# Attention scores of a two-layer mixer: products on two row tiles of 64 partitions instead of full-height products of 96

## The chip, the cores and the metric

The kernel runs on one core of a Trainium2 chip. The metric is device time of one execution in microseconds (us), the median of several executions. A core has five engines with an instruction stream each: TensorE (PE in the profile; PEld is its weight load, which is a row of its own), VectorE (DVE), ScalarE (ACT), GpSimd (POOL) and SyncE (SP), which here issues the DMAs. Engines wait for one another by semaphores.

## The reference, cut to what matters

Two layers work on 2048 latent and 256 context tokens of width 1024. The first is a convolution with a state-space scan. The second is multi-head attention with 16 heads: a head's query and key have 64 channels without position (`nope`) and 32 rotary channels (`rope`), and the rotary channels of the key are shared by all heads. The 2048 latent queries attend to all 2304 keys, 18 blocks of 128.

```python
q = jnp.concatenate([q_nope, q_rope], axis=-1)            # 64 + 32 channels
k = jnp.concatenate([k_nope, k_rope_of_all_heads], axis=-1)
...
s = jnp.einsum('bqhd,bkhd->bhqk', qblk, k, preferred_element_type=F32) * scale
p = jax.nn.softmax(s, axis=-1)
return jnp.einsum('bhqk,bkhv->bqhv', p.astype(v.dtype), v)
...
out_l = (att_l.reshape(b_, n, MLA_MIX) * jax.nn.silu(g_l)) @ w_out
```

## The kernel before

The change touches the attention of the second layer. Single precision is had from split operands: a number is a rounded high part and a low part, and `mm3` makes a product from three matmuls, high by high, high by low and low by high. Queries, keys and values, already split, lie in DRAM (`qd`, `qrd`, `kd`, `krd`, `vd`) before the attention starts.

The work runs over 64 pairs of a head and a block of 512 queries. For each pair, `NP` = 9 steps run over two key blocks of 128 each, so there are 64 x 9 = 576 steps. The loop at the end of the kernel writes each engine's instructions in that order by hand (a manual schedule); a step holds work of several lags:

- `scores`: for each of the two key blocks one `mm3` into its bank of the PSUM tile `s` (lines 119 to 121). The weights are a key block [96, 128], the moving operand is the query block [96, 512]. These are six matmuls of 96 rows and 512 columns.
- `evac_s` (ACT copies `s` to `S`, L1929), `run_max` (DVE, L1941), then 12 to 16 steps later `sub` (DVE, L1970), `exp_` (ACT, L1975), `p_hi` (ACT or POOL, L1985, L1983), `p_lo` (POOL, L1991).
- `pv`: 18 short half-precision matmuls of the probabilities by the values into `O` (L2011).
- in step 1 of a pair `max_a`, four transposes (L1951), in step 3 `max_b`, four more (L1965). `finish` divides by the row sum (DVE, L2018 to L2025; POOL, L2027).
- `side()`: at the three `side_step` calls of a step it yields one `mm3` of 512 columns into `fps`: gates and output projections. A job is 8, 4 or 2 such products with one `at` tile, which is fetched from DRAM one job ahead.

`load_k` brings a head's keys in three tiles `K` of six blocks, in steps 1, 4 and 7 of the pair before the head changes; there are four buffers. `load_qt` brings a query block one pair ahead. Each of the two issues two DMAs, one for the 64 nope rows and one for the 32 rope rows, with high and low parts side by side in a tile. All these DMAs stand in the one queue of SP, in order.

Of the kernel before, what the change touches and what calls it, by code (L numbers as in the profile page):

```python
# [10 lines left out]
F32 = mybir.dt.float32  # L11
F32R = mybir.dt.float32r
# [3 lines left out]
ALU = mybir.AluOpType  # L16
# [4 lines left out]
P = 128  # L21
# [12 lines left out]
NOPE = 64  # L34
ROPE = 32
QD = 96
VH = 64
QL = 384
# [19 lines left out]
def hybrid_conv_s5_mla_kernel(tc, x, c, ctx, c_ctx, mod_w, mod_b, norm_w, e_w_in, e_conv_w, e_lam_re, e_lam_im,  # L58
                              e_log_step, e_b_re, e_b_im, e_c_re, e_c_im, e_d, e_glu_w, e_glu_b, e_w_out,
                              o_w_in, o_q_a_norm, o_w_uq, o_kv_a_norm, o_w_ukv, o_q_norm, o_k_norm, o_w_out,  # L60
                              rope_tab, out, dbg=None):
    nc = tc.nc
    dbg = dbg or {}
    V, S, GP, PE, SP = nc.vector, nc.scalar, nc.gpsimd, nc.tensor, nc.sync
# [5 lines left out]
    with ExitStack() as top:  # L70
# [18 lines left out]
        qd = dt("qd", [2, P, 2, 4, NT])  # L89
        qrd = dt("qrd", [P, 2, 4, NT])  # L90
        kd = dt("kd", [2, P, 2, 4, TOK])
# [9 lines left out]
        def dma(out, in_, eng=None):  # L101
            (eng or SP).dma_start(out=plain(out), in_=plain(in_))
# [15 lines left out]
        def mm3(ps, lh, ll, rh, rl, start, stop):  # L118
            PE.matmul(ps, lh, rh, start=start, stop=False)  # L119
            PE.matmul(ps, lh, rl, start=False, stop=False)  # L120
            PE.matmul(ps, ll, rh, start=False, stop=stop)  # L121
# [1178 lines left out]

        def load_k(g, h, p, cuts=((0, KP),)):

            t = big.tile([P, 4, QL], F32R, name="K", bufs=4).rearrange("p a n -> p (a n)")
            t = t[0:QD].rearrange("p (a n) -> p a n", a=2)
            kt_[g, h].append(t)
            for n, (c0, c1) in enumerate(cuts):
                if n:
                    yield
                cs = slice((p * KP + c0) * P, (p * KP + c1) * P)
                ts = slice(c0 * P, c1 * P)  # L1310
                dma(out=t[0:NOPE, :, ts], in_=kd[h // 8, 64 * (h % 2):64 * (h % 2) + 64, :, h % 8 // 2, cs])
                dma(out=t[NOPE:QD, :, ts], in_=krd[:, :, cs].rearrange("a r n -> r a n"))

        def load_qt(t, h, qb):
            cs = slice(qb * 512, (qb + 1) * 512)
            dma(out=t[0:NOPE], in_=qd[h // 8, 64 * (h % 2):64 * (h % 2) + 64, :, h % 8 // 2, cs])
            dma(out=t[NOPE:QD], in_=qrd[32 * (h % 4):32 * (h % 4) + 32, :, h // 4, cs])

        man = ExitStack()
        with ExitStack() as pb:  # L1320
# [320 lines left out]
            for p in range(2):  # L1641
                run_all(load_k(0, 0, p))
            k_last = load_k(0, 0, 2, ((0, KP - 1), (KP - 1, KP)))
            qt[0] = big.tile([P, 4, QL], F32R, name="K", bufs=4).rearrange("p a n -> p (a n)")[0:QD, 0:1024]
            qt[0] = qt[0].rearrange("p (a n) -> p a n", a=2)
            load_qt(qt[0], 0, 0)
            weave(b_up(17), b_heads(16), wait=4, more=(5, 7))
            run_all(fg)
# [3 lines left out]
        with ExitStack() as at_:  # L1652
# [184 lines left out]
            def turner():  # L1837

                for l0_, l1_, k0, k1, every in ((0, 8, 0, 4, 12), (0, 8, 4, 8, 6), (8, 16, 0, 4, 7), (8, 16, 4, 6, 4),
# [3 lines left out]
                    for lt in range(l0_, l1_):  # L1843
                        while now[0] < max(ready[lt // 4, k] for k in range(k0, k1)) or (now[0] + 5) % NP < 2:
                            yield
                        a = wk.tile([P, 512], F32, name="ta", bufs=3)
                        gt = wk.tile([P, 512], F32, name="tg", bufs=2)
                        dma(out=a[:, :kn * P], in_=ad[lt, :, cs])
                        dma(out=gt[:, :kn * P], in_=gd[lt, :, cs])
# [58 lines left out]

            def load_q(i):
                g, h, qb = its[i]  # L1910
                qt[i] = wt.tile([QD, 2, 512], F32R, name="q", bufs=2)
                load_qt(qt[i], h, qb)

            def scores(i, p):
                g, h, qb = its[i]
                st = state.setdefault(i, {})
                q = qt[i]
                ps = s_p.tile([P, 2, 512], F32, name="s", tag="s")
                for a in range(2):
                    c_ = 2 * p + a  # L1920
                    K = kt_[g, h][c_ // KP]
                    cs = slice(c_ % KP * P, (c_ % KP + 1) * P)
                    mm3(ps[:, a], K[:, 0, cs], K[:, 1, cs], q[:, 0], q[:, 1], True, True)
                st["ps", p] = ps

            def evac_s(i, p):
# [87 lines left out]
            def finish(i):  # L2014
                g, h, qb = its[i]
                O = state.pop(i)["O"]
                rl = wk.tile([P, 4, 1], F32, name="rl")
                V.reciprocal(out=rl[:, :, 0], in_=O[:, VH::VW])  # L2018
                if h % 2 == 0:
                    apair[qb] = wk.tile([P, 4, 2, VH], F32, name="A%d" % (qb % 2), bufs=1)  # L2020
                ap_ = apair[qb]
                ob = wk.tile([P, 3, VW], F32, name="ob", bufs=1)
                V.tensor_tensor(out=ob, in0=O[:, 0:3 * VW].rearrange("p (r n) -> p r n", r=3),
                                in1=rl[:, 0:3].to_broadcast([P, 3, VW]), op=ALU.mult)
                V.tensor_scalar(out=ap_[:, 3, h % 2, :], in0=O[:, 3 * VW:3 * VW + VH], scalar1=rl[:, 3], scalar2=None,  # L2025
                                op0=ALU.mult)
                (V if i == NI - 1 else GP).tensor_tensor(out=ap_[:, 0:3, h % 2, :], in0=ob[:, :, 0:VH], in1=ob[:, :, VH + 1:],  # L2027
                                                         op=ALU.add)
                if h % 2 and (qb < 2 or h < NH - 1):
                    c0 = (h // 2) * P  # L2030
                    later(1, "post", lambda: dma(out=ad[4 * qb:4 * qb + 4, :, c0:c0 + P].rearrange("t p n -> p t n"),
                                                 in_=ap_.rearrange("p t a n -> p t (a n)")))
# [198 lines left out]
```

## Time and profile before

| | |
|---|---|
| median of 3 runs | 3535.63 us (3535.01 to 3538.75) |
| profiled execution, its own time | 3544.93 us |
| its span | 3542.9 us |
| busy share of the span: PE, DVE, ACT, POOL | 92%, 74%, 62%, 61% |
| attention, 1712 to 3480 us: PE, ACT, DVE, POOL busy | 1686, 1576, 1549, 1512 of 1768 us |

A busy share is the time in which an engine had at least one instruction in flight. Matmuls overlap: one of 512 columns is 0.39 us long, but the next starts 0.23 us after it, so the pace of PE is read from starts, not from lengths. The profiled execution is 9.3 us longer than the median.

### The profile page before, as it was taken

The numbers are of one execution on the slowest core, as the hardware profiler recorded it, in microseconds if no ns is written. First come the engines' busy times: TensorE is split into PE (matmuls) and PEld (weight loads), VectorE is DVE, ScalarE is ACT, GpSimd is POOL, SyncE is SP. The second block draws the span as 40 slices with busy tenths as digits, with TensorE's granted clock in tenths as the row PEclk, the third lists the DMA queues.
The fourth block names the chain that finished last, engine by engine and source line by source line (L and its number), as shares of the span: only waits on it lengthen the run. The fifth ranks groups of instructions, "written<-read, shape, count | busy, mean of one in ns | idle before, by whom it ended". The sixth has DMA issues, their size and how long they took to land. (4 is left out here: it accounts for less than half of the span.)

```text
span 3542.9 us, 63798 instructions
## 1 busy us (share of the span) xinstructions
PE 3241.8 (92%) x24725; PEld 2702.8 (76%) x24725; DVE 2633.4 (74%) x3974; ACT 2187.5 (62%) x2889; POOL 2153.3 (61%) x1347
## 2 busy tenths in 40 slices
PE   5988999989889888888799998999989999899897
PEld 4877877777767778888588887888868788688786
DVE  5766328483367676666688887888898988989897
ACT  4211322221333354444599999999989899899895
POOL 2455022222465323233388889888888988899996
PEclk9998999999999999999899999999999999899998
DMA  7333856654576656776843444445356555366584
GB/s 198 118 103 103 269 143 166 185 157 136 167 245 225 200 122 158 161 164 147 217 120 105 129 125 132 147 135 152 105 154 200 169 140 158 101 188 184 158 251 140
DMA packets 487517, 564.89 MB, mean 159 GB/s; under 512 B 83443, under 2 KB 353224, under 8 KB 479152
## 3 DMA queue, kind: packets, MB, share of 16 engines
q1 hardware_dynamic: 476080, 543.97, 54.6%
q0 software_dynamic: 2688, 8.46, 0.7%
q10 hardware_dynamic: 8448, 8.39, 0.7%
q8 instruction: 196, 3.21, 0.4%
q14 instruction: 105, 0.86, 0.1%
HBM read 378.17 MB, written 182.54 MB: 158 GB/s over the span
## 5 line engine op out<-in xcount | busy, mean ns | idle before, releaser
L1991 POOL TENSOR_TENSOR pl<-S,ph 128x1024 f16<-128x1024 f32 x430 | 918.0, 2159 | 14.5 <-ACT ph L1985 13.8
L1970 DVE TENSOR_TENSOR S<-S,t 128x1024 f32<-128x1024 f32 x432 | 520.6, 1211 | 36.9 <-PE t L1965 35.7
L1941 DVE TENSOR_TENSOR rm<-s,rm 128x1024 f32<-128x1024 f32 x384 | 468.5, 1220 | 81.0 <-ACT S L1929 62.5
L1975 ACT ACTIVATE S<-S,psh 128x1024 f32<-128x1024 f32 x432 | 498.6, 1154 | 48.1 <-DVE S L1970 47.9
L319 PE MATMUL accps<-aT,wh 128*128 128x480 f32 (+2 forms) x1920 | 491.2, 386 | 8.1 <-ACT wh L113 6.3
L119 PE MATMUL s<-q,K 96*128 96x512 f32 x1134 | 462.2, 408 | 39.4 <-DVE rm L1941 29.2
L1929 ACT COPY S<-s 128x1024 f32<-128x1024 f32 x432 | 435.5, 1008 | 58.1 <-PE s L121 53.8
L120 PE MATMUL s<-q,K 96*128 96x512 f32 x1134 | 452.3, 399 | 0.0
L121 PE MATMUL s<-q,K 96*128 96x512 f32 x1134 | 451.2, 398 | 0.0
L2011 PE MATMUL O<-Vy,ph 128*128 128x129 f16 (+2 forms) x5760 | 441.3, 211 | 0.0
L319 PEld LDWEIGHTS accps<-aT,wh 128*128 128x128 f32 x1920 | 343.2, 193 | 73.0 <-issue 18.0
L2011 PE MATMUL O<-Vy,pl 128*128 128x65 f16 x4608 | 338.2, 196 | 39.0 <-POOL pl L1991 27.4
L2011 PEld LDWEIGHTS <-pl 128*128 128x128 f16 x4608 | 242.9, 99 | 162.0 <-issue 84.2
L1985 ACT CAST ph<-S 128x1024 f16<-128x1024 f32 x288 | 302.4, 1050 | 18.7 <-PE O L2011 14.2
L1991 POOL TENSOR_TENSOR pl<-Sy,ph 128x1024 f16<-128x1024 f32 x142 | 305.3, 2170 | 7.9 <-DVE ph L1981 4.1
L2011 PEld LDWEIGHTS <-ph 128*128 128x128 f16 x5760 | 289.5, 99 | 0.0
L119 PEld LDWEIGHTS s<-q,K 96*128 96x128 f32 x1134 | 216.8, 191 | 94.6 <-DVE rm L1941 19.7
L319 PE MATMUL accps<-aT,wl 128*128 128x480 f32 (+2 forms) x960 | 265.5, 374 | 8.5 <-POOL wl L116 8.5
L121 PEld LDWEIGHTS s<-q,K 96*128 96x128 f32 x1134 | 216.7, 191 | 48.9
L120 PEld LDWEIGHTS s<-q,K 96*128 96x128 f32 x1134 | 218.1, 192 | 46.0
L116 POOL TENSOR_TENSOR wl<-w,wh 128x1024 fp32r<-128x1024 f32 x25 | 61.6, 2465 | 256.7 <-ACT wh L113 237.9
L319 PEld LDWEIGHTS accps<-aT,wl 128*128 128x128 f32 x960 | 175.4, 192 | 37.6 <-POOL wl L116 9.8
(509 smaller groups left out, 7314.6 us busy)
## 6 DMA issues: line engine op xcount, KB each, us to landing
at<-a1d SPq DMA_DIRECT2D x47, 1024.0 KB
K<-kd SPq DMA_DIRECT2D x101, 384.0 KB
w<-in_e_w_in_dram SPq DMA_DIRECT2D x48, 512.0 KB
at<-atd SPq DMA_DIRECT2D x48, 512.0 KB
Vy<-vd SPq DMA_DIRECT2D x34, 580.5 KB
K<-krd SPq DMA_DIRECT2D x101, 192.0 KB
mw<-in_mod_w_dram SPq DMA_DIRECT2D x64, 256.0 KB
a1d<-at SPq DMA_DIRECT2D x16, 1024.0 KB
```

Source lines behind the costliest of these rows:

```text
L116: el.tensor_tensor(out=lo, in0=src, in1=hi.bitcast(F32), op=ALU.subtract)
L119: PE.matmul(ps, lh, rh, start=start, stop=False)
L120: PE.matmul(ps, lh, rl, start=False, stop=False)
L121: PE.matmul(ps, ll, rh, start=False, stop=stop)
L319: PE.matmul(a_[:, 0:(j1 - j0) * q], lw[:, k, :], rt[:, k, j0 * q:j1 * q], start=(k == 0 and lw is wh and rt is aT[0]), stop=(k == KD - 1 a ...
L1929: S.copy(out=st["S", p], in_=st["ps", p])
L1941: V.tensor_tensor(out=rm, in0=ps, in1=st["S", 0] if p == 1 else rm, op=ALU.max)
L1970: V.tensor_tensor(out=sb, in0=sb, in1=state[i]["mb"][:, None, :].to_broadcast([P, 2, 512]), op=ALU.subtract)
L1975: S.activation(out=sb, in_=sb, func=AF.Exp, scale=scale, bias=psh[:, 0:1])
L1985: S.copy(out=st["ph", p], in_=st["S", p])
L1991: e.tensor_tensor(out=st["pl", p], in0=st["S", p], in1=st["ph", p], op=ALU.subtract)
L2011: PE.matmul(part(r_, v.shape[-1]), w[:, a, r_ * P:(r_ + 1) * P], v, start=(c_ == 0 and n == 0), stop=(c_ == 17 and n == 8), skip_group_che ...
```

## The change

Keys and queries now fill all 128 partitions in two halves of 64. The upper half holds the even key blocks, the lower half the odd ones. A key tile has four slots: nope high, nope low, rope high, rope low, where the 32 rope rows stand twice, one copy under the other. A query tile has three slots: nope high, nope low, and rope with the high part in the first 32 rows and the low part in the next 32, so that one matmul of 64 rows makes a rope product by both parts of the query; both halves hold the same query. `scores` is five rounds of two matmuls of 64 rows, one on each half, each into its own bank of `s`: ten matmuls instead of six.

To hold the larger query tile, `ta` goes from three to two buffers, and in `finish` the tile `ob` becomes smaller: the division of 387 columns is split in two of 192, one of them straight into its place.

```diff
@@ -1300,21 +1300,30 @@
 
         def load_k(g, h, p, cuts=((0, KP),)):
 
-            t = big.tile([P, 4, QL], F32R, name="K", bufs=4).rearrange("p a n -> p (a n)")
-            t = t[0:QD].rearrange("p (a n) -> p a n", a=2)
+
+            t = big.tile([P, 4, QL], F32R, name="K", bufs=4).rearrange("p b (c n) -> p b c n", n=P)
             kt_[g, h].append(t)
+            ks = slice(p * KP * P, (p + 1) * KP * P)
+            kn = kd[h // 8, 64 * (h % 2):64 * (h % 2) + 64, :, h % 8 // 2, ks].rearrange("r s (c a n) -> r s c a n", a=2, n=P)
+            kr = krd[:, :, ks].rearrange("s r (c a n) -> r s c a n", a=2, n=P)
             for n, (c0, c1) in enumerate(cuts):
                 if n:
                     yield
-                cs = slice((p * KP + c0) * P, (p * KP + c1) * P)
-                ts = slice(c0 * P, c1 * P)
-                dma(out=t[0:NOPE, :, ts], in_=kd[h // 8, 64 * (h % 2):64 * (h % 2) + 64, :, h % 8 // 2, cs])
-                dma(out=t[NOPE:QD, :, ts], in_=krd[:, :, cs].rearrange("a r n -> r a n"))
+                for a in range(2):
+                    c2 = slice((c0 + 1 - a) // 2, (c1 + 1 - a) // 2)
+                    if c2.start == c2.stop:
+                        continue
+                    for s in range(2):
+                        dma(out=t[64 * a:64 * a + 64, s, c2], in_=kn[:, s, c2, a])
+                        for d in range(2):
+                            dma(out=t[64 * a + 32 * d:64 * a + 32 * d + 32, 2 + s, c2], in_=kr[:, s, c2, a])
 
         def load_qt(t, h, qb):
             cs = slice(qb * 512, (qb + 1) * 512)
-            dma(out=t[0:NOPE], in_=qd[h // 8, 64 * (h % 2):64 * (h % 2) + 64, :, h % 8 // 2, cs])
-            dma(out=t[NOPE:QD], in_=qrd[32 * (h % 4):32 * (h % 4) + 32, :, h // 4, cs])
+            for a in range(2):
+                dma(out=t[64 * a:64 * a + 64, 0:2], in_=qd[h // 8, 64 * (h % 2):64 * (h % 2) + 64, :, h % 8 // 2, cs])
+                for s in range(2):
+                    dma(out=t[64 * a + 32 * s:64 * a + 32 * s + 32, 2], in_=qrd[32 * (h % 4):32 * (h % 4) + 32, s, h // 4, cs])
 
         man = ExitStack()
         with ExitStack() as pb:
@@ -1641,8 +1650,8 @@
             for p in range(2):
                 run_all(load_k(0, 0, p))
             k_last = load_k(0, 0, 2, ((0, KP - 1), (KP - 1, KP)))
-            qt[0] = big.tile([P, 4, QL], F32R, name="K", bufs=4).rearrange("p a n -> p (a n)")[0:QD, 0:1024]
-            qt[0] = qt[0].rearrange("p (a n) -> p a n", a=2)
+            qt[0] = big.tile([P, 4, QL], F32R, name="K", bufs=4).rearrange("p a n -> p (a n)")
+            qt[0] = qt[0].rearrange("p (a n) -> p a n", a=3)
             load_qt(qt[0], 0, 0)
             weave(b_up(17), b_heads(16), wait=4, more=(5, 7))
             run_all(fg)
@@ -1843,7 +1852,7 @@
                     for lt in range(l0_, l1_):
                         while now[0] < max(ready[lt // 4, k] for k in range(k0, k1)) or (now[0] + 5) % NP < 2:
                             yield
-                        a = wk.tile([P, 512], F32, name="ta", bufs=3)
+                        a = wk.tile([P, 512], F32, name="ta", bufs=2)
                         gt = wk.tile([P, 512], F32, name="tg", bufs=2)
                         dma(out=a[:, :kn * P], in_=ad[lt, :, cs])
                         dma(out=gt[:, :kn * P], in_=gd[lt, :, cs])
@@ -1908,7 +1917,7 @@
 
             def load_q(i):
                 g, h, qb = its[i]
-                qt[i] = wt.tile([QD, 2, 512], F32R, name="q", bufs=2)
+                qt[i] = wt.tile([P, 3, 512], F32R, name="q", bufs=2)
                 load_qt(qt[i], h, qb)
 
             def scores(i, p):
@@ -1916,11 +1925,11 @@
                 st = state.setdefault(i, {})
                 q = qt[i]
                 ps = s_p.tile([P, 2, 512], F32, name="s", tag="s")
-                for a in range(2):
-                    c_ = 2 * p + a
-                    K = kt_[g, h][c_ // KP]
-                    cs = slice(c_ % KP * P, (c_ % KP + 1) * P)
-                    mm3(ps[:, a], K[:, 0, cs], K[:, 1, cs], q[:, 0], q[:, 1], True, True)
+                K = kt_[g, h][p // 3]
+                for n, (kb, b) in enumerate(((0, 0), (0, 1), (1, 0), (2, 2), (3, 2))):
+                    for a in range(2):
+                        hs = slice(64 * a, 64 * a + 64)
+                        PE.matmul(ps[:, a], K[hs, kb, p % 3], q[hs, b], start=n == 0, stop=n == 4)
                 st["ps", p] = ps
 
             def evac_s(i, p):
@@ -2019,13 +2028,14 @@
                 if h % 2 == 0:
                     apair[qb] = wk.tile([P, 4, 2, VH], F32, name="A%d" % (qb % 2), bufs=1)
                 ap_ = apair[qb]
-                ob = wk.tile([P, 3, VW], F32, name="ob", bufs=1)
-                V.tensor_tensor(out=ob, in0=O[:, 0:3 * VW].rearrange("p (r n) -> p r n", r=3),
-                                in1=rl[:, 0:3].to_broadcast([P, 3, VW]), op=ALU.mult)
+                o = ap_[:, 0:3, h % 2, :]
+                ob = wk.tile([P, 3, VH], F32, name="ob", bufs=1)
+                O3 = O[:, 0:3 * VW].rearrange("p (r n) -> p r n", r=3)
+                for y, x_ in ((o, O3[:, :, 0:VH]), (ob, O3[:, :, VH + 1:])):
+                    V.tensor_tensor(out=y, in0=x_, in1=rl[:, 0:3].to_broadcast([P, 3, VH]), op=ALU.mult)
                 V.tensor_scalar(out=ap_[:, 3, h % 2, :], in0=O[:, 3 * VW:3 * VW + VH], scalar1=rl[:, 3], scalar2=None,
                                 op0=ALU.mult)
-                (V if i == NI - 1 else GP).tensor_tensor(out=ap_[:, 0:3, h % 2, :], in0=ob[:, :, 0:VH], in1=ob[:, :, VH + 1:],
-                                                         op=ALU.add)
+                (V if i == NI - 1 else GP).tensor_tensor(out=o, in0=o, in1=ob, op=ALU.add)
                 if h % 2 and (qb < 2 or h < NH - 1):
                     c0 = (h // 2) * P
                     later(1, "post", lambda: dma(out=ad[4 * qb:4 * qb + 4, :, c0:c0 + P].rearrange("t p n -> p t n"),
```

On PE, in the middle of the attention, a step with a side product stood like this in the kernel before: the last of the 18 `pv` matmuls, the side product into `fps`, six score matmuls, and the next `pv`.

```order
L2011 MATMUL O<-Vy,ph 128x129
L119 MATMUL fps<-t_14961,at 128x512
L120 MATMUL fps<-t_14962,at 128x512
L121 MATMUL fps<-t_14961,at 128x512
L119 MATMUL s<-q,K 128x512
L120 MATMUL s<-q,K 128x512
L121 MATMUL s<-q,K 128x512
L119 MATMUL s<-q,K 128x512
L120 MATMUL s<-q,K 128x512
L121 MATMUL s<-q,K 128x512
L2011 LDWEIGHTS pl
L2011 MATMUL O<-Vy,pl 128x65
```

The same place with the change:

```order
L2020 MATMUL O<-Vy,ph 128x129
L119 MATMUL fps<-t_14790,at 128x512
L120 MATMUL fps<-t_14791,at 128x512
L121 MATMUL fps<-t_14790,at 128x512
L1932 MATMUL s<-q,K 128x512 x10
L2020 LDWEIGHTS pl
L2020 MATMUL O<-Vy,pl 128x65
```

Nothing has moved around the block; in it ten matmuls on 64 rows stand for six on 96, between neighbours of full height on both sides.

On SP, where a key tile is fetched (`K`, from `kd` and `krd`), with the next side operand `at` behind it, the kernel before had:

```order
L102 DMA K<-kd 64x2x768
L102 DMA K<-krd 32x2x768
L102 DMA at<-a1d 128x2048
```

and the changed kernel has:

```order
L102 DMA K<-kd 64x3x128
L102 DMA K<-krd 32x3x128 x2
L102 DMA K<-kd 64x3x128
L102 DMA K<-krd 32x3x128 x2
L102 DMA K<-kd 64x3x128
L102 DMA K<-krd 32x3x128 x2
L102 DMA K<-kd 64x3x128
L102 DMA K<-krd 32x3x128 x2
L102 DMA at<-a1d 128x2048
```

Two DMAs have become twelve, in pieces of 128 columns, and what stands behind them in the queue comes later. A query block takes six DMAs instead of two.

## Rows read from the trace of the kernel before

**Rows 1.** Busy time by engine in stretches (us, busy and count), clock, DMA share.

```profile
1712.00:3480.00 1768.00, 1685.95 (x15614) 1365.02 (x15612) 1549.23 (x1645) 1576.36 (x1640) 1511.86 (x898) 0.98 0.53 152
...
1800.00:2000.00 200.00, 199.76 (x1884) 162.97 (x1881) 171.19 (x180) 183.91 (x190) 169.66 (x99) 1.00 0.42 124
```

**Rows 2.** Chain that ended last, 2000 to 2030 us, shares by line.

```profile
by line: PE O L2011 24.2%; PE s L120 16.2%; PE s L121 16.1%; PE s L119 16.1%; PE fps L119 9.5%; PE fps L121 7.8%; PE fps L120 7.8%; PE t L1965 1.5%; PE fps L1951 1.5%
```

**Rows 3.** Groups of instructions in the attention: busy us, mean ns, idle before.

```profile
L119 PE MATMUL fps<-t,at 128*128 128x512 f32 x240 | 114.2, 476 | 0.3
...
L119 PE MATMUL fps<-v,at 128*128 128x512 f32 x128 | 60.7, 474 | 0.1
L119 PE MATMUL fps<-u,at 128*128 128x512 f32 x112 | 53.0, 473 | 0.0
...
L1951 PE MATMUL fps<-idf,rm 128*128 128x128 f32 x252 | 39.3, 279 | 0.0
L1965 PE MATMUL t<-idf,mx 128*128 128x128 f32 x252 | 38.3, 274 | 0.0
```

**Rows 4.** Timeline of PE and PEld in one step: start us, length us.

```profile
2004.77 0.40 PE L121 MATMUL fps<-t,at 128*128 128x512 f32 x1
2005.01 0.39 PE L119 MATMUL s<-q,K 96*128 96x512 f32 x1
...
2006.16 0.40 PE L121 MATMUL s<-q,K 96*128 96x512 f32 x1
2006.40 0.30 PE L2011 MATMUL O<-Vy,pl 128*128 128x65 f16 x4
...
2004.19 0.19 PEld L119 LDWEIGHTS fps<-t,at 128*128 128x128 f32 x1
2004.30 0.19 PEld L120 LDWEIGHTS fps<-t,at 128*128 128x128 f32 x1
...
2004.78 0.19 PEld L119 LDWEIGHTS s<-q,K 96*128 96x128 f32 x1
```

**Rows 5.** Timeline of PE where L182 uses four column tiles (128*32).

```profile
622.39 0.29 PE L966 MATMUL s5ps<-R,wmq 128*128 128x144 f32 x1
622.61 0.41 PE L182 MATMUL psm<-mw,cond 128*32 128x128 f32 x6
...
622.76 0.27 PE L182 MATMUL psm<-mw,cond 128*32 128x128 f32 x1
622.96 0.50 PE L319 MATMUL accps<-aT,wh 128*128 128x512 f32 x1
...
623.30 0.40 PE L319 MATMUL accps<-aT,wh 128*128 128x512 f32 x1
```

**Rows 6.** Timeline of PEld at the same place: the weights of those tiles.

```profile
622.62 0.14 PEld L182 LDWEIGHTS psm<-mw,cond 128*32 128x32 f32 x6
```

**Rows 7.** Timeline of PE at a transpose on 32 rows (L476).

```profile
86.94 0.31 PE L319 MATMUL accps<-aT,wl 128*128 128x320 f32 x1
87.18 0.24 PE L476 MATMUL w2ps<-idf,s5ar 32*128 32x32 f32 x1
```

**Rows 8.** Waits, 1800 to 3400 us: total us, times, longest.

```profile
PEld L2011 <- POOL pl L1991: 57.1, 110, 3.6
...
PE O L2011 <- DVE A L2025: 1.4, 1, 1.4
```

**Rows 9.** Instructions of tile K on SP's queue: ns min/median/max.

```profile
L102 SPq DMA_DIRECT2D K<-kd x103: 512/527/1686, 1702.0 to 3449.2; - x103
```

**Rows 10.** Timeline of SP at the start of the attention.

```profile
1705.12 0.61 SPq L102 DMA_DIRECT2D K<-qrd  x1
1712.16 0.39 SPq L102 DMA_DIRECT2D vd<-Vy  x1
```

**Rows 11.** The DVE instructions of finish: ns min/median/max.

```profile
L2023 DVE TENSOR_TENSOR ob<-O,rl x64: 560/561/562, 1791.9 to 3527.3; 128x387 f32<-128x387 f32 x64
L2025 DVE TENSOR_SCALAR A<-O,rl x64: 273/276/277, 1792.4 to 3527.8; 128x64 f32<-128x64 f32 x64
```

## The prediction

> **What bounds the kernel now.** I first read the busy times by stretch. The attention takes 1768 us for 576 steps, 3.07 us a step. PE is in flight for 1686 us of it, ACT for 1576; where PE is fullest, from 1800 to 2000 us, ACT has 184 of 200 [rows 1]. So PE leads, with ACT 8% behind it, and that bounds any gain. The chain of waits says the same: in a stretch of 30 us it runs through PE alone, half of it through the score products, the rest through `pv`, side products and transposes [rows 2]. The groups give the number of steps with a side product: 240 + 128 + 112 first products [rows 3], 480 in all; the other 96 steps stand where side weights are split, and there PE waits for other engines. `max_a` and `max_b` follow the scores directly in 126 steps (252 transposes of each kind, four a step) [rows 3].
>
> Then I read starts on the timeline. Six score products start in 1.39 us, 0.232 us apart; each is 0.39 us long, and the weights of the next begin loading the moment the one before starts, so they are hidden [rows 4]. Two loads in a row start 0.11 us apart [rows 4]: that is what a load costs where nothing hides it.
>
> **What a change of tile shape costs.** The reader should look longest at [rows 5]. `L182` uses the array as four column tiles of 32, and its neighbours use all of it. After the last full product (622.39 us, 0.29 long) the first tile product starts at 622.61, which is 0.07 before that product's end. On the way back it is the same: a tile product from 622.76, 0.27 long, and the next full one at 622.96, again 0.07 before the end. That one is 0.50 us long where the next is 0.40, and its successor starts 0.34 after it: 0.11 for weights that could not be loaded ahead, and 0.23 of pace. A row tile of 32 rows is entered in the same way (86.94 + 0.31 against 87.18) [rows 7]. So at a change of tile shape PE lets the old products run out to 0.07 us before their end and starts loading weights only then. Between 128 and 96 rows nothing of this is seen: the first score weights load 0.01 us after the start of the side product before them [rows 4].
>
> No row shows a steady use of 64 rows, and here the rows could be read in two ways: like 96 rows, which costs nothing, or like 32. I take 32 rows as the nearest row: it is a row tile with 128 weight columns, as the new ones are. The Trainium skill speaks for the same reading: "TensorEngine Tiling (Array Packing)", Tiling Modes, says that a change of the tiling mode, though not of the tile within a mode, drains TensorE, and it lists 64 x 128 as a mode of its own. By that rule the sum is the one below; by the rows for 96 alone it would be that of the first rival.
>
> Two tiles side by side I read from the column tiles: six of their products, each some 0.28 us long, fit into 0.41 us, and the eighth starts 0.15 after the first [rows 5]. Their weights also load ahead, six within 0.14 us [rows 6]. So I take a round of two matmuls at the pace of one, 0.232 us, with 0.01 between the two. The bounds are 0.01 and a full 0.232 between them.
>
> **The change part by part.**
>
> *Entry*, per step. The first score product used to start 0.23 us after the last side product. Now it waits to 0.07 before that product's end, 0.40 - 0.07 = 0.33, and then 0.11 for its weights: 0.44. That adds 0.21 (lower bound 0, as with 96 rows).
>
> *Rounds.* From the first to the last score product there were five paces, 1.16 us; now four and the second tile, 0.94. That saves 0.22.
>
> *Exit.* `pv` used to start 0.23 after the last score product; now 0.39 - 0.07 = 0.32, so 0.09 is added. `pv` weights load in a few hundredths of a us; transposes have full weights, so in the 126 steps 0.11 more is added (lower bound 0).
>
> Sum: 0.21 - 0.22 + 0.09 = 0.08 us a step (0.076 before rounding). In 480 steps this is 36 us, and 126 x 480/576 = 105 steps with transposes give 105 x 0.11 = 12, together 48. In the 96 other steps PE waits anyway; I take nothing for them (if that cover were gone, 7 us). Part of the exits is hidden: `pv` already waits 110 times for POOL's `pl` [rows 8]; with 0.09 each, up to 10 us. That leaves 38.
>
> *DMAs.* One `K` issue holds SP for 0.53 us [rows 9]. Twelve instead of two are 5.3 us more per key tile, and six instead of two for a query 2.1 us more. Behind them stand the side operands `at`. They are fetched a job ahead, which is four steps or 12 us for a job of four, so a delay of 5 us stays hidden but for the jobs of two (6 us): 0 to 10 us, and I take 0. At the start of the attention it is not hidden. Six loads stood between 1702 and 1705.7 us, then SP was idle until 1712.2 [rows 10]; now there are 30, some 13 us more, which is 6 beyond that idle time, and the third key tile behind them adds 5 more. Writes of the last keys and queries, on which first scores hang, are in that queue. I take 10 us (0 to 20). The bytes of a key tile grow by a third; with DMA engines busy at 0.53 [rows 1] that is covered, except at the start, where it is part of the 20.
>
> *`finish`.* DVE's 387 columns took 0.56 us, 64 took 0.28 [rows 11], so 192 should take 0.39; two of them make 0.22 more, 14 us over 64 pairs. `pv` waited for this division once, 1.4 us in all [rows 8], since a block of scores lies between; I cost it at 0, and at 14 if that cover goes. `ta` with two buffers: a tile lives five steps, and in the tightest phase a new one comes every third, so its load is released in step five for step six and needed in step nine. I cost that at 0 too.
>
> Total: 38 + 10 = 48 us. On the profiled 3544.9 that is 3593; on the median, 9.3 us lower, 3584.
>
> **The rivals.**
>
> *Row tiles of 64 come and go without draining (faster).* Then a step loses 0.22 us of PE, 480 x 0.22 = 107 us. ACT, at 92% where PE is full [rows 1], would be at 99% with all of that, so I give it two thirds, 70, less 10 for the start: 3475. The rows for 96 speak for it, the rows for 32 against it. "TensorE: Matmul & The Clock Gate", Part 3 of the Trainium skill, has matmuls in distinct row groups run concurrently, as the column tiles here do, and gives no price for coming and going. It decides if entry and exit together cost under 0.2 us a step.
>
> *The weights of a pair load one after the other.* Two loads of 0.11 still fit into a round of 0.232, but the entry gets 0.11 longer: 480 x 0.11 = 53 us more, 3637. The column tiles' loads speak against it, though they are short.
>
> *Rounds do not overlap.* If the halves run one after the other, a step gains 5 x 0.22 = 1.1 us, 480 steps 530 us, about 4110. If instead the weights of a half could not load under its own product, each further round would start as after a change of shape, 0.44 instead of 0.23, 4 x 0.21 x 480 = 400 us, about 3980. The Trainium skill speaks for the latter ("TensorE: Matmul & The Clock Gate", Part 3: weight loads overlap products in flight only where row groups differ); the trace does not agree, since score weights load under a product on the same rows.
>
> *Nothing to be seen.* If the waits of `pv` for POOL and of the scores for DVE take up the whole 38 us, and SP's queue costs nothing at the start, the time stays within 0.2%, about what a measurement of this kernel can tell from no change.
>
> **How the numbers follow.** The forecast has a chance of 0.60, no drain 0.14, loads one by one 0.10, rounds that don't overlap 0.06 and nothing to be seen 0.10. The likeliest gives 3584, with its own range 3550 to 3625 from the bounds for the start, the queue, `finish` and the hidden exits. For 8 in 10 the range goes from 3480, inside the first rival, to 3650, above the second; it leaves out the 0.06 and half of the 0.14, and a remainder of the others. Faster 0.14; same 0.11; slower 0.60 + 0.10 + 0.06, less 0.01 for a forecast that ends lower, 0.75.
>
> **What the changed profile would show.** If I am right: the first of ten score matmuls starts about 0.33 us after the side product before it and is 0.11 longer than those that follow; pairs start within 0.01, rounds 0.23 apart; `pv` starts 0.32 after the last; a step with a side product takes about 0.08 us more than before; PE's chain stays. Wrong would be a first score matmul 0.23 after its neighbour (no drain; then ACT fills up), pairs 0.23 apart, or score products that wait for `K` in steps 0, 3 and 6, which would put the loss into SP's queue.

## The result, and the profile after

The changed kernel takes 3673.6 us (median of 4 executions, 3668.4 to 3691.1) where the kernel before takes 3535.3 us on the same chip. The ratio is 1.0399 with the interval [1.0362, 1.0436]: 4% slower, 138 us. The forecast was 3584 us. The direction was right, the size was not, and the time lies above the range of 3480 to 3650.

The page of the changed kernel, its span and its chain by engine and by line:

```profile
span 3667.9 us, 70046 instructions
...
PE 60%; DVE 14%; POOL 8%; DMA 8%; issue 4%; ACT 3%; SPq 3%; POOLq 0%; DVEq 0%; ACTq 0%
PE s L1932 16%; PE accps L319 10%; PE O L2020 9%; POOL pl L2000 4%; PE fps L119 3%; SPq L102 3%; PE fps L121 3%; PE fps L120 3%; DMA at<-atd 2%; PE s5ps L966 2%; PE accA L120 2%; PE accA L121 2%; PE accA L119 1%; PE accB L121 1%; PE accB L119 1%
```

PE leads the chain. The transfers of `at` have 2% of it and SP's queue 3%. (Of DMA's 8% half stand ahead of the attention. The chain of before is no measure for this, since it could be followed through only half of the span.) To place the loss I read from both traces when ACT begins its copy of the scores of step k. The lag is after minus before, in the two profiled executions (the profiled one of before is 9.3 us above its median, so a lag at the end reads some 9 us lower than the difference of the medians):

```
step                 18     270    288    324    432    540    575
lag of after, us   12.7    33.2   29.5   44.8   58.6   86.9  124.6
```

Between steps 280 and 291 the side work pauses and turns from gates to output projections. The loss has three parts: 12.7 us at the start; 20.5 us over the 252 steps 18 to 270, which is 0.081 us a step; and 95 us from step 288 on. (In the pause 3.7 us come back.) The first two are the forecast's terms (10 us, and 0.08 us a step). Of the third some 15 us are the change of shape again (the lag grows so much from step 288 on in the run below whose key tile takes four DMAs); the rest is not in the forecast.

**The change of shape, as forecast.** Timeline of PE, then PEld, of the changed kernel in one step (start us, length us). The rows answer to [rows 4]:

```profile
2011.85 0.40 PE L121 MATMUL fps<-u,at 128*128 128x512 f32 x1
2012.17 0.50 PE L1932 MATMUL s<-q,K 64*128 64x512 f32 x2
2013.21 0.39 PE L1932 MATMUL s<-q,K 64*128 64x512 f32 x2
2013.53 0.32 PE L1974 MATMUL t<-idf,mx 128*128 128x128 f32 x1
...
2012.17 0.19 PEld L1932 LDWEIGHTS s<-q,K 64*128 64x128 f32 x2 [0.36 <-issue]
2012.28 0.42 PEld L1932 LDWEIGHTS s<-q,K 64*128 64x128 f32 x4
```

The first pair starts 0.32 us after the last side product began and is 0.50 us long, where the last pair is 0.39. From the first pair to the last are 1.04 us, so with the 0.11 us of exposed weights taken off four rounds are 0.23 us apart. The first transpose starts 0.32 us after the last pair. The weights of the second round load from 2012.28, while the first pair still runs on the same rows. So weights load ahead within a half, and a rule of the Trainium skill that the prediction weighed ("TensorE: Matmul & The Clock Gate", Part 3: loads overlap only where row groups differ) is not borne out here either. The rule of "TensorEngine Tiling (Array Packing)", Tiling Modes, that a change of mode drains the array, agrees with the 0.32 us at both ends.

**The second half.** Windows of the kernel before, first and second half of the attention (us, then busy time and count of PE, PEld, DVE, ACT and POOL, then PE's granted clock, DMA share, GB/s):

```profile
1712.00:2600.00 888.00, 847.81 (x7751) 685.50 (x7750) 752.74 (x796) 788.50 (x823) 730.48 (x430) 0.98 0.47 136
2600.00:3480.00 880.00, 838.14 (x7867) 679.52 (x7865) 796.49 (x850) 787.86 (x817) 781.38 (x469) 0.98 0.59 169
```

The same of the changed kernel:

```profile
1712.00:2630.00 918.00, 869.47 (x8912) 609.58 (x8914) 742.97 (x809) 789.74 (x818) 732.35 (x427) 0.97 0.54 154
2630.00:3600.00 970.00, 874.38 (x8966) 615.45 (x8964) 789.81 (x874) 787.86 (x812) 780.11 (x464) 0.95 0.62 178
```

In the second half PE is idle for 970.0 - 874.4 = 96 us, where it was 42; and it is busy 36 us longer, at a lower granted clock (0.95 after 0.98). Waits of the changed kernel, 1800 to 3600 us (total us, times, longest):

```profile
PE fps L119 <- DMA at<-atd: 53.0, 21, 5.6
PEld fps L119 <- DMA at<-atd: 47.5, 17, 5.8
```

The kernel before has no such wait from 1800 us on. So the idle time that is new is the wait for the side operand `at`. One of these waits, first on SP's queue of the changed kernel:

```profile
2610.54 0.59 SPq L102 DMA_DIRECT2D K<-kd  x1
2611.18 1.06 SPq L102 DMA_DIRECT2D K<-krd  x2
...
2628.21 1.05 SPq L102 DMA_DIRECT2D q<-qrd  x2
2629.30 0.55 SPq L102 DMA_DIRECT2D at<-atd  x1
```

then in the chain (start us, length us, what):

```profile
2629.30 4.96 DMA at<-atd
```

then on PE, whose idle time before an instruction and its releaser stand in brackets:

```profile
2629.18 1.42 PE L1932 MATMUL s<-q,K 64*128 64x512 f32 x10
...
2631.02 0.40 PE L2020 MATMUL O<-Vy,ph 128*128 128x65 f16 x5
2634.30 0.50 PE L119 MATMUL fps<-t,at 128*128 128x512 f32 x1 [2.88 <-DMA at<-atd]
...
2635.26 2.50 PE L1932 MATMUL s<-q,K 64*128 64x512 f32 x10
```

and the window behind it:

```profile
2634.20:2637.70 3.50, 3.40 (x14) 1.98 (x14) 0.00 (x0) 0.13 (x1) 0.23 (x1) 0.62 0.98 348
```

SP issues key and query DMAs from 2610.5 to 2629.3 with almost no gap, and only then `at`, which lands 5 us later. PE stands still for 2.88 us. When it goes on, the granted clock of the next 3.5 us is 0.62, so most of them at 1.2 instead of 2.4 GHz, and the ten score products take 2.50 us instead of 1.42 us in the step before. A wait is paid twice: once as idle time and once as slower products behind it.

SP's instructions of tile `K` (ns min/median/max): the rope rows in the kernel before, which [rows 9] leave out, then both in the changed kernel:

```profile
L102 SPq DMA_DIRECT2D K<-krd x103: 319/588/1262, 1702.6 to 3449.9; - x103
...
L102 SPq DMA_DIRECT2D K<-krd x820: 302/544/2058, 1694.4 to 3582.1; - x164
L102 SPq DMA_DIRECT2D K<-kd x410: 492/580/1722, 1693.7 to 3580.8; - x137
```

A single issue costs what it did, 0.54 to 0.58 us (0.53 and 0.59 before). There are 1230 instead of 206, so some 820 x 0.544 + 410 x 0.580 = 684 us of SP's time instead of 206 x 0.56 = 115, in an attention of 1888 us (1768 before). All of SP's DMAs together take 617 of the 970 us of the second half to issue, where they took 261 of 880. How full the queue is shows in what SP waits for: the longest of its waits, in before from 1800 to 3480 us and then in after from 1800 to 3600:

```profile
SPq L102 <- PE s L121: 307.7, 90, 21.0
```

```profile
SPq L102 <- PE s L1932: 143.0, 60, 15.9
```

Before, SP arrived early and waited for PE's score products; after, it has half of that time left. From the traces I also took, for each side job of four products, the time from the issue of its `at` to its first product: 10.7 us in the median before, 7.9 after (jobs of two: 7.8 and 4.7; jobs of eight in the gates: 25.7 and 24.5).

What makes the issue late can be read from the traces too. `at` has two buffers, so its load can go out when the job two places before its own has ended. Between that moment and the issue SP spends 0.7 us in the median on issuing other DMAs in the kernel before, and 6.7 us in the changed one, of which keys and queries alone are 5.7 (jobs of two: 0.3 and 7.3). The transfer takes no longer: 4.8 us from issue to landing before, 4.9 after (jobs of two: 4.3 and 4.2).

### The profile page after: what moved, and what is told of

It is laid out like the page before. It is cut to its first block, busy times and chain, and to the rows that moved or that the text cites. A ratio compares the mean times of both kernels' runs of the same rounds, so it can differ in the third digit from the quotient of the medians.

```text
span 3667.9 us, 70046 instructions
## 1 busy us (share of the span) xinstructions
PE 3303.4 (90%) x27029; PEld 2562.3 (70%) x27029; DVE 2626.7 (72%) x4038; ACT 2196.0 (60%) x2889; POOL 2160.5 (59%) x1347
## 4 chain that ended last, share of the span: by engine, by line
PE 60%; DVE 14%; POOL 8%; DMA 8%; issue 4%; ACT 3%; SPq 3%; POOLq 0%; DVEq 0%; ACTq 0%
PE s L1932 16%; PE accps L319 10%; PE O L2020 9%; POOL pl L2000 4%; PE fps L119 3%; SPq L102 3%; PE fps L121 3%; PE fps L120 3%; DMA at<-atd 2%; PE s5ps L966 2%; PE accA L120 2%; PE accA L121 2%; PE accA L119 1%; PE accB L121 1%; PE accB L119 1%
## 5 line engine op out<-in xcount | busy, mean ns | idle before, releaser
L1932 PE MATMUL s<-q,K 64*128 64x512 f32 x5670 | 837.5, 423 | 30.4 <-DVE rm L1950 17.1
L1932 PEld LDWEIGHTS s<-q,K 64*128 64x128 f32 x5670 | 508.0, 190 | 293.4 <-issue 100.7
L1992 POOL CAST ph<-S 128x1024 f16<-128x1024 f32 x143 | 148.9, 1041 | 133.9 <-PE O L2020 107.8
L1979 DVE TENSOR_TENSOR Sy<-Sy,t 128x1024 f32<-128x1024 f32 x144 | 173.6, 1210 | 12.5 <-PE t L1974 12.5
L1491 POOL TENSOR_TENSOR Sy<-Sy,rB3y 128x1024 f32<-128x1024 f32 x15 | 28.6, 1905 | 251.1 <-DVE rB3y L134 234.6
L1984 ACT ACTIVATE Sy<-Sy,psh 128x1024 f32<-128x1024 f32 x144 | 166.2, 1154 | 13.1 <-DVE Sy L1979 13.0
```

Source lines behind the costliest of these rows:

```text
L1932: PE.matmul(ps[:, a], K[hs, kb, p % 3], q[hs, b], start=n == 0, stop=n == 4)
L1979: V.tensor_tensor(out=sb, in0=sb, in1=state[i]["mb"][:, None, :].to_broadcast([P, 2, 512]), op=ALU.subtract)
L1984: S.activation(out=sb, in_=sb, func=AF.Exp, scale=scale, bias=psh[:, 0:1])
```

## The experiments

Two theories stood at first. **Theory Q** (queue): what goes beyond the forecast is the number of DMAs in SP's queue, which brings `at` late. **Theory P** (PE): the row tiles cost more in the second half than in the first, and the waits for `at` follow from that. All ratios are against the kernel before on the same chip. The expectations also name **theory N**, which is Q made narrower (it is the number of DMAs, not their size), and **theory C** (contention: the DMA engines are slower with more and smaller pieces).

### The old products with the new number of DMAs

```diff
-                cs = slice((p * KP + c0) * P, (p * KP + c1) * P)
-                ts = slice(c0 * P, c1 * P)
...
+                for c in range(c0, c1):
+                    cs = slice((p * KP + c) * P, (p * KP + c + 1) * P)
+                    ts = slice(c * P, c * P + P)
+                    dma(out=t[0:NOPE, :, ts], in_=kd[h // 8, 64 * (h % 2):64 * (h % 2) + 64, :, h % 8 // 2, cs])
+                    dma(out=t[NOPE:QD, :, ts], in_=krd[:, :, cs].rearrange("a r n -> r a n"))
...
```

A key tile is fetched block by block, in twelve DMAs, and the query in six.

> The kernel before, with its key tile in twelve DMAs (one nope and one rope DMA for each of the six blocks, pieces of 128 columns) and its query block in six; products, bytes and layout stay. Theory Q (the queue of SP: side operands stand behind key and query DMAs): the start and the waits for side operands come with the DMAs alone, 12 + about 70 us, so 3600 to 3625. Theory P (PE: the coming and going of the 64-row tiles costs more than the 0.08 us a step of the sum): nothing, 3535 to 3545.

Measured: 3651.4 us, 1.0336 [1.0321, 1.0351]. Its waits, and its second half:

```profile
PE fps L119 <- DMA at<-atd: 59.5, 19, 6.4
PEld fps L119 <- DMA at<-atd: 56.0, 16, 6.5
```

```profile
2610.00:3575.00 965.00, 862.52 (x7785) 697.38 (x7786) 783.63 (x838) 779.05 (x806) 772.21 (x462) 0.94 0.51 156
```

The old products alone, with the new number of DMAs, lose 118 us, and 95 of the 101.8 us of lag arise after step 270. PE is idle for 102 us and its granted clock is 0.94, close to the 0.95 of the changed kernel. DMAs were busy less than in the second half of before (0.51 after 0.59). PE is also busy 24 us longer than in the second half of before, with the same products, so the slower clock costs time without any change of shape. Theory P falls. Theory Q holds, and the loss was larger than I expected of it.

### The same number of DMAs with long pieces

```diff
-                dma(out=t[0:NOPE, :, ts], in_=kd[h // 8, 64 * (h % 2):64 * (h % 2) + 64, :, h % 8 // 2, cs])
+                for r in range(0, NOPE, 8):
+                    r0 = 64 * (h % 2) + r
+                    dma(out=t[r:r + 8, :, ts], in_=kd[h // 8, r0:r0 + 8, :, h % 8 // 2, cs])
...
```

The old products again, twelve DMAs a key tile, but cut by partitions, so that a row of a DMA stays 3072 bytes long (512 in the run above).

> The kernel before, with the key tile in twelve DMAs again, but cut by partitions: eight rows each, pieces of 3072 bytes as before; queries in six. Theory N: the same loss as with twelve DMAs of short pieces, 3630 to 3660. Theory C: no loss, 3535 to 3560.

Measured: 3668.2 us, 1.0375 [1.0355, 1.0396]. Its wait for `at`:

```profile
PE fps L119 <- DMA at<-atd: 68.1, 19, 6.7
```

Longer pieces don't help, and theory C falls: the DMA engines have 498 thousand packets here, as in the kernel before (488), where the run above has 606. It is the number of DMAs.

### The new DMAs with full-height products

```diff
-                for n, (kb, b) in enumerate(((0, 0), (0, 1), (1, 0), (2, 2), (3, 2))):
-                    for a in range(2):
-                        hs = slice(64 * a, 64 * a + 64)
-                        PE.matmul(ps[:, a], K[hs, kb, p % 3], q[hs, b], start=n == 0, stop=n == 4)
+                for a in range(2):
+                    for n, (kb, b) in enumerate(((0, 0), (2 + a, 1), (1 + a, 2 * a))):
+                        PE.matmul(ps[:, a], K[:, kb, p % 3], q[:, b], start=n == 0, stop=n == 2)
```

> The changed kernel with its layout and DMAs, but the scores of a step are six products of all 128 rows, three into each bank; their values mix even and odd blocks. No change of tile shape is left, and PE's work a step is that of the kernel before. Theory Q: only the 0.08 us a step goes, about 40 to 48 us: 3625 to 3635. Theory P: 3535 to 3550.

Measured: 3650.0 us, 1.0341 [1.0322, 1.036]. By the ratios this is 0.0058, or some 20 us, better than the changed kernel (1.0399), less than expected. In the first half the lag no longer grows (13.9 us at step 18, 15.0 at 270), so there the shape change is the whole 0.08 us a step. In the second half it grows as before, to 118.3: what PE saves there, it waits longer for `at` (66.4 us instead of 53.0).

A second kernel has five such products instead of six:

```diff
-                    for a in range(2):
-                        hs = slice(64 * a, 64 * a + 64)
-                        PE.matmul(ps[:, a], K[hs, kb, p % 3], q[hs, b], start=n == 0, stop=n == 4)
+                    PE.matmul(ps[:, n % 2], K[:, kb, p % 3], q[:, b], start=n < 2, stop=n > 2)
```

> As the one with six products of 128 rows, but five, three into one bank and two into the other: what five rounds would cost if tiles came and went for nothing; a fifth of the scores' products is left out. Theory Q: PE loses another 0.23 us a step where side products run; the waits for side operands and ACT (8% behind PE) take back about half: 3560 to 3600. Theory P: 3450 to 3500.

Measured: 3602.5 us, 1.0202 [1.0185, 1.0219]. At step 288 it leads before by 25.9 us, at the end it lags by 54.8: even with a round less on PE the second half loses 80 us.

### `at` past SP's queue

```diff
...
-                    dma(out=a[:, :, k0:k1], in_=atd[lt, :, :, k0:k1])
-                    dma(out=ht, in_=hd[lt, :, ns])
+                    dma(out=a[:, :, k0:k1], in_=atd[lt, :, :, k0:k1], eng=S)
+                    dma(out=ht, in_=hd[lt, :, ns], eng=S)
```

The side loads are issued by ACT, those of the gates too. First with the load of the partial sums `ht`, as shown, then `at` alone.

> The changed kernel, with the loads of the side operands (at, and the partial sum beside it) issued from ACT's queue instead of SP's. Theory Q: the waits of side products for their operands, about 100 us before PE, go, and 60 to 80 us with them: 3595 to 3615. Theory C (contention: the DMA engines are slower with more and smaller pieces, whichever queue issues): 3660 to 3680. Theory P: 3665 to 3675.

> The changed kernel, with only the tile at issued from ACT's queue; the partial sum, whose load waits for a store and so held ACT in the run before, stays on SP. Theory N: at no longer stands behind key and query DMAs, most of the 90 us of the output projections come back: 3595 to 3625. Theory C: 3660 to 3680. Should ACT be held by something else as before, the gates' stretch shows it: over 3700.

Measured: 3801.9 us, 1.0765 [1.0749, 1.0781], and 3698.8 us, 1.0454 [1.043, 1.0479]. Both are slower than the changed kernel. What ACT waits for, in the first and then in the second of them:

```profile
ACT S L1938 <- DMA hd<-fo: 78.3, 13, 8.6
...
ACT S L1938 <- DMA out_dram<-fo: 44.3, 8, 7.6
```

```profile
ACT S L1938 <- DMA atd<-tm: 27.5, 4, 9.1
ACT S L1938 <- DMA K<-krd: 27.4, 6, 6.8
```

A load that ACT issues must wait for the store that wrote its data or freed its buffer, and that store still stands in SP's queue. ACT waits with it, and the copy of the scores behind it comes late. (What the waits for `K` in the second run stand for is not shown.) In the second run PE waits for `at` only once, 1.0 us, so `at` is in time there; but the loss moved to another engine, and neither run separates the theories by its time. They show that `at` depends on SP's queue twice, by its own place and by its writer's.

### The twelve DMAs spread over the steps

```diff
...
-                        run_all(load_k(*its[i + 1][:2], p // 3))
+                        kq.append(load_k(*its[i + 1][:2], p // 3))
+                    for _ in range((0, 1, 1, 2, 1, 1, 2, 2, 2)[p]):
+                        if kq and next(kq[0], "end") == "end":
+                            kq.pop(0)
```

`load_k` yields after every third DMA, and the loop takes one or two of these pieces a step.

> The changed kernel with the same twelve DMAs a key tile on the same queue, but spread: three or six a step instead of twelve at once. Theory N, in the form that a side operand waits for what stands just ahead of it: at most six DMAs are ahead, 3600 to 3630. Theory N in the form that SP is simply too full: 3655 to 3675. Theory C: 3660 to 3675.

Measured: 3663.4 us, 1.036 [1.0341, 1.0379]. Its wait for `at`, 53.0 in the changed kernel:

```profile
PE fps L119 <- DMA at<-atd: 44.0, 17, 4.6
```

The intervals of the two ratios overlap, so a gain in time is not shown; by the medians it would be some 10 us. The bunch that stands right ahead of an `at` is at most a small part of the loss. The rest comes with the queue as a whole.

### Fewer DMAs: keys laid out in DRAM as the tile wants them

```diff
+        def kcol(kt):
+            return (kt // KP * KP + kt % 2 * (KP // 2) + kt % KP // 2) * P
...
-                    for s in range(2):
-                        dma(out=t[64 * a:64 * a + 64, s, c2], in_=kn[:, s, c2, a])
-                        for d in range(2):
-                            dma(out=t[64 * a + 32 * d:64 * a + 32 * d + 32, 2 + s, c2], in_=kr[:, s, c2, a])
+                    dma(out=tv[hs, 0:2, l0:l1], in_=kd[h // 8, 64 * (h % 2):64 * (h % 2) + 64, :, h % 8 // 2, k0 + l0:k0 + l1])
+                    dma(out=tv[hs, 2:4, l0:l1], in_=krd[:, :, k0 + l0:k0 + l1].rearrange("s r n -> r s n"))
...
```

The writers of `kd` and `krd` store even blocks ahead of odd ones, and the rope rows twice, so that a key tile needs four DMAs instead of twelve. The products are those of the changed kernel.

> The changed kernel, with keys laid down in DRAM in the order in which the tile wants them (the even blocks of a tile, then the odd ones, rope rows twice), so that a key tile takes four DMAs of long pieces instead of twelve; row tiles stay. Theory N (number of DMAs in SP's queue): the waits for side operands nearly go, and what stays is the change of tile shape, about 40 us, and a few us at the start: 3575 to 3600. Theory C (size of the pieces, load of the DMA engines): the pieces are still half of those before and the bytes a third more, so part stays: 3610 to 3650.

Measured: 3576.5 us, 1.0117 [1.0101, 1.0133]. Its waits, second half and SP's longest wait:

```profile
PEld fps L119 <- DMA at<-atd: 3.2, 2, 2.0
PE fps L119 <- DMA at<-atd: 2.9, 2, 1.8
```

```profile
2618.00:3510.00 892.00, 846.03 (x8990) 598.11 (x8988) 790.89 (x878) 788.54 (x815) 781.61 (x467) 0.98 0.70 191
```

```profile
SPq L102 <- PE s L1934: 261.2, 87, 18.6
```

The waits for `at` are all but gone, the granted clock is 0.98 again, PE is idle for 46 us (42 before) and busy 8 us longer. `at` is issued 10.6 us ahead of its job, as before. DMAs are busier than in any kernel above (0.70), so their share was not what brought `at` late. The lag at step 18 is 0.7 us, so the start was the queue as well. From here to the changed kernel are 1.0399 - 1.0117 = 0.0282, or 100 us: the price of the eight DMAs more a key tile.

Then the same with the six full-height products of above:

> Keys in DRAM in the tile's order (four DMAs a key tile), but six score products of all 128 rows, values mixed: the changed kernel without change of tile shape and nearly without the longer queue. Theory D (what is left in the run with four DMAs, 44 us, is the going in and out of the 64-row tiles): 3535 to 3548. Rival F (it is what the other parts brought: the split division, ta with two buffers, six query DMAs, a third more bytes): 3565 to 3580.

Measured: 3542.2 us, 1.0012 [1.0001, 1.0023]. The third more bytes, six query DMAs, the split division and the smaller `ta` cost 4 us together (0 to 8 by the interval). So what is left in the run before is the shape: 1.0117 - 1.0012 = 0.0105, or 37 us, with 30 to 44 from the two intervals.

And with five full-height products, which is what five rounds would take if the row tiles came and went for nothing:

> Keys in DRAM in the tile's order, five score products of 128 rows (a fifth of the scores' products left out, values mixed): five rounds without any change of shape, the first rival of the prediction. If PE leads and ACT is the next bound, 0.23 us of PE a step bring 50 to 80 us against the kernel before: 3455 to 3490.

Measured: 3470.5 us, 0.9819 [0.9796, 0.9843]. Its first half, where ACT is as full as PE:

```profile
1712.00:2540.00 828.00, 775.44 (x7399) 622.94 (x7399) 729.36 (x796) 776.22 (x812) 721.09 (x421) 0.98 0.60 165
```

ACT is busy for 776 of 828 us, PE for 775. A product less is worth 68 us (1.0012 - 0.9819 = 0.0193), where 480 paces of 0.232 us would be 111. The rest is lost to the other engines: besides a full ACT, PE's products wait 76 us for POOL's `pl` (1800 to 3500 us), where they waited 22 in before. Which of the two sets the pace was not tested. From this run to the one on row tiles are 0.0298, or 105 us: coming and going costs more than the round that it saves. No kernel here with all of the products is faster than the kernel before.

### Half as many changes of shape

```diff
-                    scores(i, p)
+                    if t % 2 == 0:
+                        scores(i, p)
+                        scores(*divmod(t + 1, NP))
...
+                for m_ in (t - 1, t) if t % 2 and t <= total else ():
+                    evac_s(*divmod(m_, NP))
+                    run_max(*divmod(m_, NP))
...
```

The scores of two steps stand in one block of twenty matmuls, so that the array changes shape half as often; ACT's copies come a step later. It is done to the kernel with keys in tile order, and to the kernel before as a control.

> Keys in DRAM in the tile's order, row tiles, and the scores of two steps issued in one block of twenty matmuls every second step, their evacuation one step later: half as many changes of tile shape. Theory D: a step's going in and out falls from 0.30 to 0.15 us, the saving of the rounds stays 0.22; 0.07 us a step below the kernel before: 480 x 0.07 = 34 us, 3495 to 3530, if ACT and DVE stand the burst. Rival F: no better than the run with four DMAs, 3565 to 3590.

> The control: the kernel before, with the scores of two steps in one block of twelve products. There is no change of tile shape to save, so theory D expects nothing, 3528 to 3550, or a loss if the bursts make PE wait for ACT and DVE. Should it gain as much as the row tiles do, the gain of those is not from the changes of shape.

Measured: 3670.1 us, 1.0375 [1.0359, 1.0391], and the control 3680.7 us, 1.0408 [1.0391, 1.0425]. The pairing itself costs 144 us: ACT and DVE did not stand the burst, the condition of the first expectation. Two waits of the control:

```profile
ACT S L1975 <- DVE S L1970: 91.2, 132, 2.3
ACT S L1929 <- POOL pl L1991: 87.7, 63, 3.4
```

The other engines get their work in bursts, and wait for one another. But within the pairing the row tiles are 0.0033, or 12 us, faster than the old products, where without it they were 0.0117, or 41 us, slower. Half of the changes away moved them by 53 us; by the rows, 0.15 us in 480 steps, it would be 72. PE bounds these two less (busy 548 and 558 us from 1800 to 2400, after 590 in before), so part of what it gains or loses can be hidden: the sign speaks for theory D, the size is no clean measure of it.

## Why the prediction was wrong

**Right: what bounds the kernel.** PE led: in the first half and in the run with four DMAs a tile, what PE lost came out in the time. Of the 111 us that a product less would save, 68 came out, since the other engines stand close behind.

**Right: the change of shape.** Entry, rounds and exit are read off the timeline as they were put. The step lost 0.081 us in the first half (forecast 0.08 and transposes, less hidden exits), and the runs with four DMAs a tile put the whole at 37 us where the forecast had 38.

**Right: `finish` and `ta`, at nothing.** The two halves of the division, to be held against [rows 11], are 0.36 and 0.35 us:

```profile
L2035 DVE TENSOR_TENSOR A<-O,rl x64: 356/357/359, 1805.5 to 3652.2; 128x192 f32<-128x192 f32 x64
L2035 DVE TENSOR_TENSOR ob<-O,rl x64: 345/347/352, 1805.8 to 3652.5; 128x192 f32<-128x192 f32 x64
```

Together they are 0.14 us longer than the one division, where the forecast had 0.22. The run with six full-height products and four DMAs a tile puts it, `ta` and two other parts at 4 us together.

**Right: the start**, 12.7 us at step 18 against 10, and 0.7 with four DMAs a tile. In single executions of the other runs with twelve it is 5 to 18, so that the two agree so closely is luck.

**Wrong: "Behind them stand the side operands `at`. ... 0 to 10 us, and I take 0."** This is the step that failed. It measured 100 us less the 12 of the start, some 88. Three things in it were wrong, and the first two could have been worked out from the trace of before:

- The lead was put at four steps or 12 us, all of it free. It is 10.7 us in the median from issue to first product, and the transfer takes 4.8 of them. For a job of two it is 7.8, and the transfer takes 4.3. So a job of two has 3.5 us to spare, a job of four 6.
- The delay was put at one key tile's 5.3 us. SP's issues stood with almost no gap for 18.8 us in the rows above, since the loads of two tiles and a query ran into one another. Cost per issue was right; the sum over the queue was not made.
- The wait was taken as the whole price. PE's clock fell behind it: in the second half PE was idle for 54 us more and busy for 36 us more, of which the shape explains 8.

The clock accounts for the 28 us that are left. By the clock records of the traces PE is busy for 83 us of the second half at 1.2 GHz, and for 25 in the run with four DMAs a tile; at the other level, 2.4 GHz, the 58 us between them would take half as long, so I estimate 29 us. Of the 83 us 48 lie in stretches of the low clock that begin at a wait for `at`; the kernel before has 36 in all, behind other waits.

The profile that the prediction named as proof against it was waits for `K`. It came as waits for `at`, behind the `K` loads in the same queue: right queue, wrong victim.

**The rivals.** The first (no draining, 3475) did not occur: the first pair starts 0.32 us after its neighbour, not 0.23. Its 70 us for the saved round were well priced, 68 measured; that 3475 and the 3471 of five full-height products lie so close is partly luck, since the 10 us for the start, which the rival counts, are not in that run. The second falls with the weights of the first pair, which load together in 0.19 us. Rounds did overlap, 0.23 us apart, and the loss is far from nothing.

**What stays open.** That `at` is late by SP's own time for issuing, and not by late stores that its load waits for, is read from the traces (6.7 instead of 0.7 us of issuing ahead of it) and not separated by a run: both runs that moved loads to ACT held ACT. In the second half the shape's price hardly shows in the time of the changed kernel, since PE waits longer for `at` when its products are cheaper. Row tiles of other heights were not tried.

## What to carry to other kernels

An in-order DMA queue is an engine: add up its issues before and after (here 115 us of keys in 1768, and 684 in 1888) and not only the delay of one bunch, and ask which load behind it has the shortest lead once the transfer's own time is taken off. A layout in SBUF that takes more DMAs is better made where the data are written to DRAM, once, than at each of many loads. Packing products on row tiles saves rounds but pays 0.30 us for coming and going, so one saved round of 0.23 us for each entry is not enough.

## What the runs showed of the hardware

- Twelve DMAs a key tile cost as much in pieces of 3072 bytes (1.0375) as of 512 (1.0336): the count decided.
- The third more bytes of a key tile cost at most a part of 4 us, at a DMA share of 0.71 of the second half (2600 to 3480 us, six full-height products and four DMAs a tile).
- Between full-height products and two row tiles of 64 the next product started 0.32 us after the last, both ways, instead of 0.23, and the first pair was 0.50 us long instead of 0.39. Within the tiles rounds stood 0.23 us apart, and weights loaded under products on the same rows.
- Loads that ACT issued held it up to 9.1 us at a time, behind a store in another queue.
- After an idle time of 2.88 us PE's granted clock was 0.62 for 3.5 us, and ten score products took 2.50 us instead of 1.42.
